# Moving four modulation tiles of layer 2 into an expert stage, with smaller bias tables and a later query factor

## Chip, cores and metric

One core of one Trainium2 chip runs the whole program. The metric is the device time of one execution in microseconds; lower is better. TensorE (PE), VectorE (DVE), ScalarE (ACT), GpSimd (POOL) and SyncE (SP) each run their own instruction stream in order, and wait for one another by semaphores. SP and ACT also issue DMA transfers from their streams.

## What is computed

Two blocks of two layers each work on 256 tokens of 1024 numbers, in float32. Every layer is a mixer (an attention or a gated scan) followed by 16 experts of which each token uses two. In block 1, `c` modulates both halves of a layer:

```
cond = silu(c)
for l in range(2):
    mod = cond @ w_ada[l] + b_ada[l]
    sh1, sc1, g1, sh2, sc2, g2 = split(mod, 6)
    h = layer_norm(x) * (1 + sc1) + sh1
    x = layer_norm(ALPHA * x + g1 * mixer(h), ln1_g[l], ln1_b[l])
    h = layer_norm(x) * (1 + sc2) + sh2
    x = layer_norm(ALPHA * x + g2 * moe(h), ln2_g[l], ln2_b[l])
```

`mod` has 6144 numbers, twelve tiles of 512. Tiles 0 to 3 (`sh1`, `sc1`) are needed when a layer begins. The mixer of block 1 normalizes queries and keys by head, turns them by position ("rope") and scales scores by 1/8. The second layer of block 2 adds a bias by relative position, looked up in a table of 32 buckets, to its scores.

## The kernel before

Everything is unrolled; a scheduler puts each engine's instructions in order. The text order is its priority, `after_last(engine)` keeps an instruction behind the last one written for that engine, and `chain_begins` to `chain_ends` marks stretches that keep the written order. The stages follow one another: layer 1 of block 1, its experts (tag `moe10`), layer 2, its experts (`moe11`), then block 2 with `moe20` and `moe21`.

**A layer of block 1** (`block1`) multiplies the tokens by weights in 28 units: 20 of `w_in`, 4 of the branches, 4 of `w_out`. Weights come as 1 MB tiles into a ring of eight. Each is split into a high part on ACT (`whi`, L346) and a low part on DVE (`wlo`, L356), and a unit is 48 matmuls of 128x128 by 128x256 (L427). After every 12 of these, `Flow.tick` resumes the side tasks: the lane `job` holds rope, `att` the attention, and `ada` the modulation.

**The modulation** of one tile (`ada_task`) loads 2 MB in two transfers on SP's queue, then sums the eight slices of it on DVE into `adac`: one multiplication (L520) and seven multiply-adds (L522). For tiles that are needed as columns, four narrow products on PE (L529) and one addition on DVE (L532) end it; for the gate rows `g1` and `g2` it is one product of 128x512 (L534) and an addition (L536). The lane begins after a pause of 12 ticks (`ADA_START`). In layer 1 it takes tiles 4 to 11 of its own layer, then tiles 0 to 3 of layer 2, then a folding of the router's weights. Before the units of `w_out` the lane is drained: whatever is left of it is written there, in front of the residual. The first `w_out` units are computed by `residual`, with `ot` (L1018) as the first step of its DVE chain, and behind the merged branches (`mt`, L1501 to L1505).

**Rope** (L1296 on) has POOL raise the mean square to the power -1/2 (`rstd_of`, L203). For the queries DVE then multiplies the result `rq` by 0.125 (L1309), ahead of the rotation (`sq` on DVE, `o2` on POOL, `qro` as their sum, L1327) and the transposes (L1333). `rq` itself is used only in the softmax of `global_job`.

**An expert stage** (`moe`) gathers the tokens of four experts at a time (`pg`, L334), then works on pairs of experts: `up` (L786), `act`, `down` (L850), and `land`, which spreads the results (`sc`) and adds them to `X` (L892). Weight tiles of 1 MB are loaded ahead into the ring, into ten more slots of the same size that lie where the layer's own tiles were, and into two work tiles; `PLAN1` gives their order. In the middle of the stage (`OV_AT`) every engine takes a branch (L907) around code for experts with more than 64 tokens. Places marked by `hint_for` tell an engine beforehand where that branch leads; for `moe10` the short engines have one mark, at the very start of the program, and PE has two more inside the stage.

**The bias table** is made by `bias_task` in layer 2: eight rows of 384 numbers, each written 128 times to the DRAM tile `fd` (L1542), so that `diff` can read it back shifted by one number per partition, in two transfers (L1783).

Of the kernel before, what the change touches and what calls it, by code (L numbers as in the profile page):

```python
# [91 lines left out]

RING = 8
TICK = 12
ADA_START = (12, 12)

TAIL_ENG = (ENG.Activation, ENG.PE)
WARM = ((3, 2, 10), (3, 2, 10))
# [7 lines left out]
def _plan(places, fixed):  # L106

    turns = [i for i in range(len(places)) if i not in fixed.values()]
    return [(p, fixed[p] if p in fixed else turns.pop(0)) for p in (("ring" if p == "r" else p) for p in places)]


PLAN1 = _plan([5, 6, 7] + ["r"] * 8 + [9, 8, 1, 2, 3, 4, 0, "yy"], {"yy": 8})
SLOTS1 = (1, 9, PLAN1, 99), (1, 9, PLAN1, 99)
FIX2 = {"sa": 3, "yy": 17}
SLOTS2 = ((3, 8, _plan([3, "r", "r", 8, 9, 4, 5, 6, "r", "r", "r", 7, 10, "r", "r", "r", "yy", 1, 2, 0, "sa", "rows"], FIX2), 14),
          (3, 8, _plan([8, 9, 3, "r", 5] + ["r"] * 7 + [4, 6, 10, 7, "yy", 1, 2, 0, "sa", "rows"], FIX2), 14))
SM_TICKS = 4
JOB_GAP = 2
P_BUFS = 4
S_BANKS = 3  # L120
DEC = 4
TAGS = ("moe10", "moe11", "moe20", "moe21")
# [8 lines left out]
def body(ctx: ExitStack, tc: tile.TileContext, A: dict, out: bass.AP, dbg=None):  # L131
# [377 lines left out]
    def ada_task(ps, pool, l, m, step):  # L509

        src = kview(A["w_ada"][l], m * 512, (m + 1) * 512)
        if m not in MODC:
            b = A["b_ada"][l, m * 512:(m + 1) * 512]
            g = gates[l, m // 6][:, (m % 2) * 512:(m % 2) * 512 + 512]
            S.dma_start(g, bass.AP(tensor=b.tensor, offset=b.offset, ap=[[0, P], [1, 512]]))
        ws = [wload([4, 512], [(None, src[:, 4 * i:4 * i + 4])]) for i in range(2)]
        yield 2
        acc = pool.tile([P, 512], F32, tag="adac", name="adac", bufs=1)
        with after_chain():
            V.tensor_scalar(acc, ws[0][:, 0], ce[:, 0:1], None, op0=OP.mult)  # L520
        for k in range(1, KC):
            V.scalar_tensor_tensor(acc, ws[k // 4][:, k % 4], ce[:, k:k + 1], acc, op0=OP.mult, op1=OP.add)  # L522
            if k % step == 0:
                yield 1
        yield 1
        pa = ps.tile([P, 512], F32, tag="tp", name="pa", bufs=2)
        if m in MODC:
            for j in range(4):
                PE.matmul(pa[:, j:j + 1], acc[:, j * 128:(j + 1) * 128], one32[:, 0:1], start=(j == 0), stop=(j == 3),  # L529
                          skip_group_check=True)  # L530
            yield 1
            V.tensor_tensor(modc[l][:, MODC[m]:MODC[m] + 4], pa[:, 0:4], modc[l][:, MODC[m]:MODC[m] + 4], op=OP.add)  # L532
        else:
            PE.matmul(pa, one32, acc, start=True, stop=True)  # L534
            yield 1
            V.tensor_tensor(g, pa, g, op=OP.add)  # L536


    def rank4(mp, v, n, tag):
# [106 lines left out]
        else:  # L646
            V.tensor_copy(cb[:, 1], pb[:, n:2 * n])

    def moe(z, kind, slots, scored, wg, wu, wd, mod, gate, tag, after, again, reorder=False, room=()):

# [4 lines left out]
        with ExitStack() as es:  # L657
# [298 lines left out]
            gx = gather(0)  # L956
            pos_sb = mo.tile([P, 48], F32, tag="pos", name="pos_sb")
            V.tensor_copy(pos_sb, pos[:, 0:48])
            ga = act(0, *up(0, gx))
            if reorder:  # L960
                with after_last(ENG.Activation):
                    S.dma_start(X, xd.rearrange("(t p) d -> p t d", p=P))
            for pi in range(8):
                if pi in (OV_AT - 3, OV_AT - 1):
                    with after_last(ENG.PE):
                        tc.mark_branch_hint_location("ov" + tag, engines=[ENG.PE])
                if pi < 7:
                    if pi % 2 == 1:
                        gx = gather(pi // 2 + 1)
                    gu = up(pi + 1, gx)  # L970
                st = ga[0]
                ys = down(pi, *ga, pi == 7)
                if pi < 7:
                    ga = act(pi + 1, *gu)
                    land(pi, 0, spread(st, *ys, 0))
                    land(pi, 1, spread(st, *ys, 1))
                if pi == OV_AT:
                    overflow()
                if pi == OV_AT + 1:
                    for e in SHORT:  # L980
                        with after_last(e):
                            hint_for(TAGS[TAGS.index(tag) + 1:], e)
                if pi == 6:
                    with after_last(ENG.Activation):
                        tail = Tail(after(), again)
                    chain_begins(*TAIL_ENG)
# [175 lines left out]
    def block1(l, prev):  # L1162

        with tc.tile_pool(name="gp", bufs=1, reuse_waits="tile") as gp:
            gates[l, 1] = gp.tile([P, D], F32, name="g2")
            es = gp.tile([P, 2, NE], F32, name="es")
            with ExitStack() as stack:
# [128 lines left out]
                def rope(src, dst, H, nm, rs, permute):  # L1296
# [8 lines left out]
                    if not permute:  # L1305
                        sv = src.rearrange("p t (h e) -> p (t h) e", e=64)
                        V.tensor_tensor(sv, sv, rs[:, :, None].to_broadcast([P, 2 * H, 64]), op=OP.mult)
                    else:
                        V.tensor_scalar(rs, rs, 0.125, None, op0=OP.mult)  # L1309
                    tA, tB = tabs[nm]  # L1310
                    o2 = d.tile([P, 2, H * 64], F32, tag="kdT", name="o2")
                    for tt in range(2):
# [12 lines left out]
                        else:  # L1325
                            o, a, b = dst[:, tt], sq[:, tt], o2[:, tt]
                        V.tensor_tensor(o, a, b, op=OP.add)  # L1327
                    for tt in range(2):
                        yield 2
                        if permute:  # L1330
                            pt = ps.tile([P, 512], F32, tag="tp", name="ptq")
                            for j in range(4):
                                PE.transpose(pt[:, j * P:(j + 1) * P], qro[:, tt, j * P:(j + 1) * P], ident)  # L1333
                            S.activation(qT[:, :, tt * P:(tt + 1) * P], pt.rearrange("p (j t) -> p j t", j=4), AF.Copy)
                        else:
                            pt = ps.tile([P, 512], F32, tag="tp", name="ptk")
                            PE.transpose(pt[:, 0:P], kro[:, tt, :], ident)
                            S.activation(kT[:, tt * P:(tt + 1) * P], pt[:, :P], AF.Copy)
# [103 lines left out]
                if ADA_START[l]:  # L1442
                    fl.add("ada", pause(ADA_START[l]))
                fl.add("ada", *[ada_task(ps, d2, l, m, ADA_STEP[l]) for m in range(4, 12)])
                fl.add("ada", *[ada_task(ps, d2, k, m, ADA_STEP[l]) for k in range(l + 1, DEPTH) for m in range(4)])
                fl.add("ada", fold(ps, d2, "adas", route, modc[l][:, 24:32], modc[l][:, 16:24], False))
                if l + 1 == DEPTH:
                    fl.add("ada", bias_task(ps, d2))
# [58 lines left out]
                def logits(tt, t, sd):  # L1507
# [4 lines left out]
                             route, logits, gates[l, 0])  # L1512
            return moe(z, 1, SLOTS1[l], (es, route[1]), A["w_exp_gate"][l], A["w_exp_up"][l], A["w_exp_down"][l],
                       (modc[l][:, 24:32], modc[l][:, 16:24]), gates[l, 1], f"moe1{l}",
                       lambda: rows_of(A["ln2_g"][l], A["ln2_b"][l], False), l + 1 < DEPTH, l + 1 == DEPTH)


    lam = cst.tile([P, 4], F32, name="lam")
    fd = dram.tile([8, P, 384], F32, name="fd")
    fap = fd[:]  # L1520

    def bias_task(ps, pool):
# [16 lines left out]
        yield 1  # L1539
        fsb = pool.tile([8, 384], F32, tag="pT", name="fsb", bufs=3)  # L1540
        V.tensor_copy(fsb, pf[0:8, :384])
        S.dma_start(fd, fsb[:, None, :].to_broadcast([8, P, 384]))  # L1542
        yield 2
        t = pool.tile([P, 128], F32, tag="adas", name="ltm")
        tc.keep_in_program_order(V.tensor_tensor(t, ab[0], ab[1], op=OP.mult))
# [194 lines left out]
    def diff(prev, gp, room, load_router, logits, rows):  # L1740
        with tc.tile_pool(name="dl", bufs=1, reuse_waits="tile") as dl, tc.tile_pool(name="d", bufs=1, reuse_waits="tile") as d, tc.tile_pool(name="d2", bufs=2, reuse_waits="tile") as d2, \
# [38 lines left out]
            v = [t[:, 0].rearrange("p (t n) -> p t n", t=2) for t in vb]  # L1780
            Tb = [t[:, 1].rearrange("p (h n) -> p h n", h=4) for t in vb]
            for i in range(2):
                S.dma_start(Tb[i], bass.AP(tensor=fap.tensor, offset=fap.offset + 127 + i * 4 * P * 384,  # L1783
                                           ap=[[383, P], [P * 384, 4], [1, 256]]))
            pbuf = slot(7, [4, 2, 256], "pbuf")
            pairs = [(0, 1), (2, 3)]
            gs = row_bcast(d, "gs", A["b_g_sub_2"][0])
# [166 lines left out]
```

## Time and profile before

| | us |
|---|---|
| three runs | 1598.65, 1603.44, 1602.59; median 1602.59 |
| the profiled execution | 1602.16 |
| its span, first to last instruction | 1600.4 |
| PE busy | 1470.0 |
| DVE busy | 869.0 |
| ACT busy | 432.8 |

The profiled execution lies 0.4 us below the median, and its span 1.8 us below its time. The mean granted TensorE clock is 0.969 of full speed. By the profile's times, layer 1 runs up to about 277 us, `moe10` to about 430 us, layer 2 to about 674 us and `moe11` to about 840 us.

### The profile page before, as it was taken

Reading aid. Unit: us, or ns where it says so; the run is one execution under the profiler, and the core shown is the slowest. Engines: PE = TensorE matmul, PEld = TensorE weight load, DVE = VectorE, ACT = ScalarE, POOL = GpSimd, SP = SyncE. Lnnn points to the kernel's source line nnn. Section 1 sums busy time; section 2 is a strip of 40 time slices with the busy share of each in tenths; the row PEclk is TensorE's granted clock in tenths of the full one; section 3 lists DMA queues with packets and bytes.
Section 4 is the critical chain, followed back from the end, with each engine's and each line's share of the span. In section 5 each row is a group of like instructions: output and inputs, shape, how many; then the busy total and the mean of one; then the engine's idle time right before and its main releaser. Section 6 shows DMA issues by size and latency. Waiting matters only on the chain. (4 is left out here: it accounts for less than half of the span.)

```text
span 1600.4 us, 22811 instructions
## 1 busy us (share of the span) xinstructions
PE 1470.0 (92%) x9124; PEld 969.4 (61%) x9124; DVE 869.0 (54%) x1686; ACT 432.8 (27%) x733; POOL 129.2 (8%) x140
## 2 busy tenths in 40 slices
PE   4999987998889999889989999999998999999895
PEld 3879987443478999734448895443337988434331
DVE  3689998343678879823464574231127776212214
ACT  1454331211235434111125331110103652101000
POOL 0200002000121000300011001000003002000001
PEclk9999999999979999889999999999999999999998
DMA  9978799995855769799887487999999966999993
GB/s 301 365 249 273 259 303 324 353 302 198 268 174 173 242 232 337 167 363 359 292 263 214 133 290 267 386 387 353 381 334 288 298 195 244 341 386 387 346 386 124
DMA packets 324371, 461.69 MB, mean 288 GB/s; under 512 B 20077, under 2 KB 178285, under 8 KB 324258
## 3 DMA queue, kind: packets, MB, share of 16 engines
q1 hardware_dynamic: 308720, 446.34, 81.5%
q10 hardware_dynamic: 15538, 13.81, 3.5%
q8 instruction: 76, 1.25, 0.3%
q14 instruction: 37, 0.30, 0.1%
HBM read 456.43 MB, written 3.67 MB: 287 GB/s over the span
## 5 line engine op out<-in xcount | busy, mean ns | idle before, releaser
L786 PE MATMUL gu<-w,xg 128*64 128x512 f32 x1536 | 369.2, 597 | 0.0
L786 PEld LDWEIGHTS gu<-w,xg 128*64 128x64 f32 x1536 | 110.8, 137 | 209.1 <-issue 202.7
L356 DVE TENSOR_TENSOR wlo<-w,whi 128x2048 fp32r<-128x2048 f32 (+2 forms) x92 | 183.3, 1994 | 44.9 <-ACT whi L346 44.2
L850 PE MATMUL y<-w,sa 128*64 128x512 f32 x768 | 195.6, 607 | 4.4 <-DMA w<-in_w_exp_down_dram 4.4
L346 ACT ACTIVATE whi<-w 128x2048 fp32r<-128x2048 f32 (+2 forms) x92 | 157.9, 1726 | 151.4 <-PE acc L427 111.6
L850 PEld LDWEIGHTS y<-w,sa 128*64 128x64 f32 x768 | 55.0, 138 | 106.0 <-issue 97.7
L830 DVE SCALAR_TENSOR_TENSOR sa<-gu,cr,sa 128x256 f32<-128x256 f32 (+1 forms) x32 | 19.7, 615 | 163.6 <-PE gu L786 136.4
L334 PE MATMUL sc<-yy,st 128*128 128x512 f32 x256 | 88.8, 436 | 18.1 <-ACT yy L860 14.3
L522 DVE SCALAR_TENSOR_TENSOR adac<-w,ce,adac 128x512 f32<-128x512 f32 x140 | 104.7, 748 | 1.2
L427 PE MATMUL acc<-hl,whi 128*128 128x256 f32 x608 | 93.3, 286 | 0.0
L427 PE MATMUL acc<-hh,whi 128*128 128x256 f32 x608 | 90.4, 289 | 1.6 <-ACT whi L346 1.6
L892 DVE TENSOR_TENSOR x<-x,sc 128x512 f32<-128x512 f32 x112 | 74.3, 683 | 30.4 <-PE sc L334 30.3
L427 PE MATMUL acc<-hh,wlo 128*128 128x256 f32 x608 | 85.9, 281 | 0.0
L334 PE MATMUL pg<-oh,zh 128*128 128x256 f32 x256 | 73.8, 319 | 13.1 <-DVEq L907 7.3
L334 PEld LDWEIGHTS sc<-yy,st 128*128 128x128 f32 x256 | 42.0, 188 | 70.7 <-ACT yy L860 36.0
L427 PEld LDWEIGHTS acc<-hh,whi 128*128 128x128 f32 x608 | 78.4, 190 | 6.8 <-issue 4.1
L427 PE MATMUL acc<-whi,hh 128*128 128x256 f32 x416 | 70.9, 303 | 12.2 <-ACT hh L1240 8.9
L427 PEld LDWEIGHTS acc<-hl,whi 128*128 128x128 f32 x608 | 79.6, 189 | 3.7 <-issue 3.2
L427 PEld LDWEIGHTS acc<-hh,wlo 128*128 128x128 f32 x608 | 77.3, 188 | 1.0 <-issue 0.8
L334 PEld LDWEIGHTS pg<-oh,zh 128*128 128x128 f32 x256 | 55.4, 218 | 27.8 <-issue 15.0
L334 PE MATMUL pg<-oh,zl 128*128 128x256 f32 x256 | 71.2, 308 | 0.9 <-issue 0.9
L860 ACT ACTIVATE yy<-y 128x512 fp32r<-128x512 f32 x32 | 19.1, 597 | 192.2 <-PE y L850 192.2
(376 smaller groups left out, 2107.8 us busy)
## 6 DMA issues: line engine op xcount, KB each, us to landing
w<-in_moe_w_gate_dram SPq DMA_DIRECT2D x64, 1024.0 KB, 12.1
w<-in_moe_w_up_dram SPq DMA_DIRECT2D x64, 1024.0 KB, 13.8
w<-in_moe_w_down_dram SPq DMA_DIRECT2D x128, 512.0 KB, 11.6
w<-in_w_ada_dram SPq DMA_DIRECT2D x47, 1024.0 KB, 7.2
w<-in_w_in_dram SPq DMA_DIRECT2D x40, 1024.0 KB, 5.6
w<-in_w_exp_gate_dram SPq DMA_DIRECT2D x64, 512.0 KB, 9.5
w<-in_w_exp_up_dram SPq DMA_DIRECT2D x64, 512.0 KB, 8.8
w<-in_w_exp_down_dram SPq DMA_DIRECT2D x64, 512.0 KB, 8.9
```

The costliest lines, as they stand in the source:

```text
L334: PE.matmul(dst, l, r, start=(i == 0), stop=(i == n - 1), skip_group_check=True)
L346: S.activation(hi[:, k0:k0 + n], w, AF.Copy)
L356: eng.tensor_tensor(lo[:, k0 + x:k0 + y], w[:, x:y], hi[:, k0 + x:k0 + y].bitcast(F32), op=OP.subtract)
L427: PE.matmul(dst, l, r, start=(start and i == 0), stop=(i == n - 1), skip_group_check=True)
L522: V.scalar_tensor_tensor(acc, ws[k // 4][:, k % 4], ce[:, k:k + 1], acc, op0=OP.mult, op1=OP.add)
L786: PE.matmul(gu[64 * j:64 * j + 64, :], xg[:, 4 * kh + k, (2 * pr + j) * CAP:(2 * pr + j + 1) * CAP], ws[j][:, k, :], start=(kh == 0 and k ...
L830: V.scalar_tensor_tensor(sg, u, cr, sg, op0=OP.mult, op1=OP.mult)
L850: PE.matmul(y[64 * j:64 * j + 64, :], aT[:, f, 64 * j:64 * j + 64], w[:, j, k, :], start=(f == 0), stop=(f == NF - 1), tile_position=(0, 6 ...
L860: S.activation(yh[:, hs], src, AF.Copy)
L892: V.tensor_tensor(X[:, tt, hs], X[:, tt, hs], sc, op=OP.add)
```

## The change

The four tiles of layer 2 leave the `ada` lane of layer 1. `ada_steps` sums them inside `moe10` instead, in 16 steps of two slices, each with a load of 0.5 MB on ACT's queue into one of two new buffers; one call starts it after the first pair, then three calls a pair for pairs 0 to 2 and two for the others. `moe10` gets one slot less ahead. In layer 2 the pause of the lane is 8 ticks in place of 12. In `ada_task` the gate rows' product comes `step` ticks later. The queries' factor stands below the rotation. `moe10` marks the branch once more after pair 1 for DVE, ACT, POOL and SP. Each row of `fd` is written 32 times instead of 128, and read in eight transfers of 32 partitions.

```diff
-ADA_START = (12, 12)
+ADA_START = (12, 8)
...
-SLOTS1 = (1, 9, PLAN1, 99), (1, 9, PLAN1, 99)
+PLAN0 = _plan([5, 6, 7] + ["r"] * 8 + [8, 1, 2, 3, 4, 0, "yy"], {"yy": 8})
+SLOTS1 = (1, 8, PLAN0, 99), (1, 9, PLAN1, 99)
...
+FD = 32
...
@@ ada_task
-        yield 1
+        yield 1 if m in MODC else step + 1
...
+    def ada_steps(ps, pool, l):
+        steps = [(m, i) for m in range(4) for i in range(4)]
+        def load(m, i):
+            w = pool.tile([P, 2, 512], F32, tag="adaw", name="adaw", bufs=2)
+            with after_last(ENG.Activation):
+                S.dma_start(w, kview(A["w_ada"][l], m * 512, (m + 1) * 512)[:, 2 * i:2 * i + 2])
+            return w
+        w = load(*steps[0])
+        yield
+        for n, (m, i) in enumerate(steps):
+            ahead = load(*steps[n + 1]) if n + 1 < len(steps) else None
+            if i == 0:
+                acc = pool.tile([P, 512], F32, tag="adac", name="adac", bufs=1)
+            with after_last(ENG.DVE):
+                for j in range(2):
+                    k = 2 * i + j
+                    if k == 0:
+                        V.tensor_scalar(acc, w[:, 0], ce[:, 0:1], None, op0=OP.mult)
+                    else:
+                        V.scalar_tensor_tensor(acc, w[:, j], ce[:, k:k + 1], acc, op0=OP.mult, op1=OP.add)
+            w = ahead
+            yield
+            if i == 3:
+                pa = ps.tile([P, 512], F32, tag="tp", name="pa", bufs=2)
+                with after_last(ENG.PE):
+                    for j in range(4):
+                        PE.matmul(pa[:, j:j + 1], acc[:, j * 128:(j + 1) * 128], one32[:, 0:1], ...
+                with after_last(ENG.DVE):
+                    V.tensor_tensor(modc[l][:, MODC[m]:MODC[m] + 4], pa[:, 0:4], modc[l][:, MODC[m]:MODC[m] + 4], op=OP.add)
...
@@ moe
+            ada = iter(()) if ada is None else ada_steps(ps, mp, ada)
             ga = act(0, *up(0, gx))
+            next(ada, None)
...
                     land(pi, 1, spread(st, *ys, 1))
+                for _ in range(3 if pi < 3 else 2):
+                    next(ada, None)
+                if pi == 1 and tag == TAGS[0]:
+                    for e in SHORT:
+                        with after_last(e):
+                            hint_for(TAGS, e)
...
@@ rope
-                    else:
-                        V.tensor_scalar(rs, rs, 0.125, None, op0=OP.mult)
...
                         V.tensor_tensor(o, a, b, op=OP.add)
+                    if permute:
+                        V.tensor_scalar(rs, rs, 0.125, None, op0=OP.mult)
...
@@ block1
-                fl.add("ada", *[ada_task(ps, d2, k, m, ADA_STEP[l]) for k in range(l + 1, DEPTH) for m in range(4)])
...
@@ bias_task, diff
-    fd = dram.tile([8, P, 384], F32, name="fd")
+    fd = dram.tile([8, FD, 384], F32, name="fd")
...
-        S.dma_start(fd, fsb[:, None, :].to_broadcast([8, P, 384]))
+        S.dma_start(fd, fsb[:, None, :].to_broadcast([8, FD, 384]))
...
-                S.dma_start(Tb[i], bass.AP(tensor=fap.tensor, offset=fap.offset + 127 + i * 4 * P * 384,
-                                           ap=[[383, P], [P * 384, 4], [1, 256]]))
+                for p0 in range(0, P, FD):
+                    S.dma_start(Tb[i][p0:p0 + FD], bass.AP(tensor=fap.tensor, offset=fap.offset + 127 - p0 + i * 4 * FD * 384,
+                                                           ap=[[383, FD], [FD * 384, 4], [1, 256]]))
```

## Rows read from the trace of the kernel before

**Rows 1.** The page's busy time by engine, whole span.
```profile
PE 1470.0 (92%) x9124; PEld 969.4 (61%) x9124; DVE 869.0 (54%) x1686; ACT 432.8 (27%) x733; POOL 129.2 (8%) x140
```

**Rows 2.** Busy time by stretch: us, engines' busy us (instructions), PEclk, DMA share, GB/s.
```profile
350.00:410.00 60.00, 55.30 (x226) 21.61 (x225) 21.81 (x39) 9.42 (x22) 1.18 (x2) 0.94 0.54 181
210.00:260.00 50.00, 41.38 (x317) 40.03 (x316) 45.84 (x89) 12.25 (x14) 1.53 (x1) 0.93 0.96 315
370.00:390.00 20.00, 15.30 (x66) 8.56 (x67) 7.93 (x14) 3.52 (x6) 1.18 (x2) 0.83 0.83 279
700.00:710.00 10.00, 7.27 (x15) 1.92 (x16) 0.92 (x2) 0.63 (x1) 0.00 (x0) 0.50 1.05 381
```

**Rows 3.** PE's waits, 190 to 252 us: total us, times, longest.
```profile
PE acc L427 <- DVE wlo L356: 2.2, 1, 2.2
PE acc L427 <- ACT mh L1504: 2.1, 1, 2.1
PE accb L427 <- DVE mt L1502: 2.0, 2, 1.6
PE acc L427 <- DVE ot L1018: 1.9, 1, 1.9
```

**Rows 4.** Instructions on the tile `adac`, 185 to 250 us: durations ns min/median/max.
```profile
L522 DVE SCALAR_TENSOR_TENSOR adac<-w,ce,adac x32: 732/747/752, 184.8 to 244.1; 128x512 f32<-128x512 f32 x32
...
L520 DVE TENSOR_SCALAR adac<-w,ce x4: 477/480/485, 191.8 to 233.4; 128x512 f32<-128x512 f32 x4
```

**Rows 5.** PE's waits, 560 to 700 us (end of layer 2's mixer).
```profile
PE acc L427 <- DVE ot L1018: 1.7, 1, 1.7
```

**Rows 6.** PE's waits, 62 to 100 us (layer 1's first units).
```profile
PE ptq L1333 <- DVE qro L1327: 2.7, 1, 2.7
PE pa L534 <- DVE adac L522: 2.2, 1, 2.2
```

**Rows 7.** Waits around the queries' rope: layer 1 (DVE), then layer 2 (PE).
```profile
DVE rq L1309 <- POOL rq L203: 2.1, 1, 2.1
...
PE ptq L1333 <- DVE g L536: 1.7, 1, 1.7
```

**Rows 8.** The branch L907 in `moe10`, and who waited for it.
```profile
L907 DVEq COMPARE_BRANCH x1: 84/84/84, 375.8 to 375.8; - x1
...
L907 DVEq EVENT_SEMAPHORE x1: 21/21/21, 381.1 to 381.1; - x1
...
  PE pg L334: 4.7, 1
```

**Rows 9.** The same branch in `moe11`, 750 to 850 us.
```profile
L907 DVEq COMPARE_BRANCH x1: 74/74/74, 784.4 to 784.4; - x1
L907 DVEq EVENT_SEMAPHORE x1: 21/21/21, 784.9 to 784.9; - x1
```

**Rows 10.** DMA queues, 645 to 680 us: packets, MB, share of 16 engines.
```profile
q10 hardware_dynamic: 1032, 1.57, 36.2%
q1 hardware_dynamic: 3295, 3.38, 31.3%
```

**Rows 11.** PE in order of time in `moe11`: start us, us, what, [idle before].
```profile
701.33 1.94 PE L850 MATMUL y<-w,sa 128*64 128x512 f32 x2 [3.00 <-DMA w<-in_w_exp_down_dram]
704.67 6.37 PE L850 MATMUL y<-w,sa 128*64 128x512 f32 x14 [1.40 <-DMA w<-in_w_exp_down_dram]
```

**Rows 12.** PE in order of time: the same products in `moe10`.
```profile
299.82 3.65 PE L850 MATMUL y<-w,sa 128*64 128x512 f32 x16
```

**Rows 13.** All DMA in `moe10`, 280 to 350 us.
```profile
DMA packets 20557, 24.92 MB, mean 356 GB/s; under 512 B 757, under 2 KB 16070, under 8 KB 20554
```

**Rows 14.** DVE in order of time in `moe10`, [idle before].
```profile
333.66 0.42 DVE L822 TENSOR_SCALAR st<-pst 128x256 fp32r<-128x256 f32 x1 [5.54 <-ACT pst L821]
```

**Rows 15.** DMA issues of the whole run: count, KB each, us to landing.
```profile
rows<-in_ln_b_dram ACTq DMA_DIRECT2D x6, 512.0 KB, 7.4
```

**Rows 16.** The two reads of `fd` (L1783): durations ns.
```profile
L1783 ACTq DMA_DIRECT2D vb<-fd x2: 378/379/380, 1178.6 to 1182.0; - x2
```

More of the change, by code (lines that the diff above doesn't have):

```diff
@@ L536, in ada_task @@
             V.tensor_tensor(g, pa, g, op=OP.add)
+    def ada_steps(ps, pool, l):
[24 more added lines that the diff above has]
+                    for j in range(4):
+                        PE.matmul(pa[:, j:j + 1], acc[:, j * 128:(j + 1) * 128], one32[:, 0:1], start=(j == 0), stop=(j == 3),
+                                  skip_group_check=True)
+                with after_last(ENG.DVE):
+                    V.tensor_tensor(modc[l][:, MODC[m]:MODC[m] + 4], pa[:, 0:4], modc[l][:, MODC[m]:MODC[m] + 4], op=OP.add)
     def rank4(mp, v, n, tag):
@@ L647, in fold, with moe @@
             V.tensor_copy(cb[:, 1], pb[:, n:2 * n])
-    def moe(z, kind, slots, scored, wg, wu, wd, mod, gate, tag, after, again, reorder=False, room=()):
+    def moe(z, kind, slots, scored, wg, wu, wd, mod, gate, tag, after, again, reorder=False, room=(), ada=None):
         F = wg.shape[2]
@@ L1514, in block1 @@
                        (modc[l][:, 24:32], modc[l][:, 16:24]), gates[l, 1], f"moe1{l}",
-                       lambda: rows_of(A["ln2_g"][l], A["ln2_b"][l], False), l + 1 < DEPTH, l + 1 == DEPTH)
+                       lambda: rows_of(A["ln2_g"][l], A["ln2_b"][l], False), l + 1 < DEPTH, l + 1 == DEPTH,
+                       ada=l + 1 if l + 1 < DEPTH else None)
     lam = cst.tile([P, 4], F32, name="lam")
-    fd = dram.tile([8, P, 384], F32, name="fd")
+    fd = dram.tile([8, FD, 384], F32, name="fd")
     fap = fd[:]
```

## The prediction

> **What bounds the kernel now.** I read the page's busy times first: PE is busy for 1470.0 of 1600.4 us, DVE for half of that [rows 1]. The kernel is bound by PE, so only PE's gaps, and stretches in which it runs below full clock, can be shortened. The next views are therefore PE's waits stage by stage, then for each gap the engine named as its releaser, in order of time, and the DMA queues where a transfer is the releaser. Four places matter.
>
> At the end of layer 1's mixer PE has gaps of 2.2, 2.1, 2.0 and 1.9 us [rows 3]. In those 50 us DVE is busy for 45.84 us, PE for 41.38, and PE's mean granted clock is 0.93 [rows 2]. Four sums of modulation tiles begin in that stretch [rows 4]; by the order of the lane they are the four of layer 2, which the drain has put in front of the residual. DVE is the bound here, for a moment.
>
> In the first units of layer 1, PE waits 2.2 us for a gate row's sum and 2.7 us for the rotated queries [rows 6], and DVE in turn had stood 2.1 us at `rq`, for POOL's power; at the same place of layer 2 PE has a gap of 1.7 us [rows 7].
>
> In `moe10` the branch costs DVE 5.3 us, from 375.8 to 381.1, and PE waits 4.7 us for what stands behind it [rows 8]. The same branch takes 0.5 us in `moe11` [rows 9].
>
> In `moe11` PE waits 3.0 and 1.4 us for one tile of `w_exp_down`, and its products then run at the lower level (granted 0.50, so 1.2 GHz) [rows 2, 11]. Just before, the write of `fd` is in flight: over 35 us ACT's queue took 36.2% of the DMA engines for 1.57 MB, while the weights in SP's queue got 3.38 MB through [rows 10]. At the rate of `moe10`, 356 GB/s [rows 13], 35 us carry 12.5 MB; only 5.0 MB moved.
>
> **The change part by part.** *The four tiles leave layer 1.* A tile costs DVE 0.48 + 7 x 0.747 = 5.7 us, four 22.8 us [rows 4], and an addition each. That is half of DVE's 45.84 us in the stretch, so DVE stops being the bound there. The PE gaps sum to 8.2 us. Layer 2's mixer ends in the same way with only its last gate tiles draining, and still shows a gap of 1.7 us [rows 5]; I leave that much, and take 6.5. The clock loss there is 0.07 x 41.38 = 2.9 us [rows 2]; part of it is owed to gaps that stay behind 250 us, so I take 1.5. Together 8.0, between 3 (DVE's splitting of weights is late without them too) and 11. The lane of layer 1 now has 12 + 4 x 7 + 4 x 9 + 2 = 78 ticks against 88 that the units give, so little is drained; before it was 98. The eight loads of 1 MB leave SP's queue, and `w_out` and the experts behind them can only come sooner.
>
> *Gate products later, the factor below the rotation.* In layer 1 the 2.2 us wait for the gate's sum goes, since the product is issued two ticks later. `rq` no longer stands ahead of `qro`, so 2.1 of the 2.7 us go; POOL has ended its power by the time that the rotation's last sum is done, and nothing waits for `rq` until the softmax. Sum 4.3, taken as 4.0, bounds 0 and 5. In layer 2 the 1.7 us gap goes: 1.5, bounds 0 and 2. What is late next is DVE itself, busy nearly throughout. Layer 2's lane starts 4 ticks sooner and each of its four gate rows ends a tick later, so it ends where it did: 0, within 1.5 either way.
>
> *The second mark for the branch.* If it does for `moe10` what the mark set a stage ahead does for `moe11`, DVE's 5.3 us become 0.5. PE's wait falls from 4.7 us to about 0.3, a gain of 4.4, and of the clock loss, 0.17 x 15.30 = 2.6 us [rows 2], about half goes, since it follows that gap: 5.5, bounds 0 and 7. Four marks cost an instruction each on engines that have room.
>
> *A quarter of `fd`.* The write fell on 36.2% of 16 engines for 35 us; a quarter of the packets is about 9 us of this, so the weights behind it come some 20 us sooner. PE could have begun the products at 701.33 - 3.00 = 698.3 and ended at 711.0, 12.7 us; in `moe10` the same sixteen take 3.65 [rows 11, 12]. The difference, 9.1 us, is the most to be had; I take 8, with 2 as the lower end in case the slot of that tile, and not the queue, holds it back. The reads become eight: six more issues of 0.38 us on ACT, 2.3 us in a stage where ACT mostly waits [rows 16]: cost 0.5, bounds 0 and 2.
>
> *The tiles' sums in `moe10`.* PE's work is only moved: the narrow products of a tile are taken from layer 1 and added here, net 0. The loads, 16 of 0.5 MB or 8.4 MB, cost 8.4 / 356 GB/s = 23.6 us of DMA [rows 13]. From 350 to 410 us the DMA share is 0.54 [rows 2], so 0.46 x 60 = 27.6 us lie free there, more than the loads need. That the engines could rest so long, while no weights are named among `moe10`'s waits, means that weights run that far ahead of PE; loads that come in before 350 us only use up this lead. They are hidden; if that cover failed, the price would be up to 23.6 us. One prefetch slot less, in other places: cost 1, bounds 0 and 3, since SP's queue is in order and a slot that comes free late holds those behind it.
>
> DVE has 22.8 us more to do, while PE computes `up`. Its gap there is 5.5 us in a pair [rows 14], and three steps of two slices take 3 x 1.5 = 4.5. But there are two buffers: the load of a burst's third step must wait on ACT until DVE has done the first. The nearest row for a 0.5 MB load from ACT's queue lands in 7.4 us [rows 15], so the third step could end 1.5 + 7.4 + 1.5 = 10.4 us into the gap, 4.9 late. What queues behind it on DVE is the next pair's `st`, `sa`, `yt` and `yy`, for which PE waits; behind the waiting load on ACT stand the next pair's Silu and its copies of `yy`. Three bursts are of three steps: bounds 0 (the scheduler puts the next pair's work ahead, or the load lands in the gap) and 14.7. A burst of two finds its second load issued ahead of the gap. I take 1 us for each of the three, 3 in all, because the scheduler orders by when it thinks data is ready.
>
> **Sum.** 8.0 + 4.0 + 1.5 + 5.5 + 8.0 - 0.5 - 1.0 - 3.0 = 22.5 us off the profiled execution's 1602.2: 1579.7. That execution lies 0.4 below the median, so the forecast for the median is **1580**.
>
> **The rivals.** *The mark changes nothing.* DVE's branch in `moe10` is missed though a mark was set, at the program's start, and the new one still stands some two pairs ahead of the branch. Against: in `moe11` a mark set longer before works [rows 9]. Then 5.5 us are lost: 1585.
> The Trainium skill (Runtime: NRT & Kernel Launch, section Instruction fetch mechanics) says that instructions are fetched one page after the other into a window of two, and that a taken branch out of that window waits for a fetch; by that rule a mark far ahead could keep nothing, and the time would be this rival's. The 0.5 us of `moe11`'s branch speaks against it as far as it goes.
>
> *The third steps are late.* All three cost their 4.9 us, and the gaps lower the clock as at 700 us, so 14.7 in place of 3: about 1592.
>
> *Slower.* The loads in ACT's queue land late for every burst: the three of three steps and the four of two. The mechanism is DVE's order: a multiply-add that waits for its load holds the next pair's `sa` and `yy`, and PE stops in every pair. All other terms give 25.5 us, so it decides from 25.5 / 7 = 3.6 us a burst. At the bound of 4.9 it costs 34 us: 1611. For it: the DMA share near 1 up to 350 us. Against: weights of the same size pass at 356 GB/s then, and DVE is idle for most of each pair.
>
> *The change doesn't free PE.* If the gaps at the end of layer 1 only move to the next wait (first loads of `moe10`, routing) and the tile of `moe11` stays late, 3 + 0 + 0 + 0 + 2 less the costs of 4.5 is about 0: 1601.
>
> **How the numbers follow.** The forecast has 0.56, the dead mark 0.24, late third steps 0.10, no freed PE 0.05, slower 0.05. About 0.3%, 5 us, is what a measurement of this kernel can tell from no change, so the line lies at 1597.8. The first three cases are faster, but for a small share of the late steps: 0.88. Within 0.3%: 0.07. Slower by more: 0.05. At their best all terms give 11 + 5 + 2 + 7 + 9.1 = 34 us, 1568. The range reaches from 1569, nearly that, to 1594, past the dead mark and the late steps; it leaves out the last two cases and a tail below, under 2 in 10.
>
> **What would show it.** In the profile of the changed kernel: no `adac` sums after about 215 us in layer 1 and no PE gap over 1 us before `ot`; `rq` behind `qro`, without DVE's wait; DVE's branch in `moe10` within 1 us; ACT's queue with about 260 packets instead of 1032 after the end of layer 2's mixer, and the sixteen products of `moe11`'s first `down` in 3.65 us. PE's waits within `moe10`, now none, tell how late the steps are. I am wrong if gaps of several us appear there in each pair, or if `moe10` begins no sooner than 277 us.

## The result and the profile after

| | before | after |
|---|---|---|
| median, us | 1603.0 (4 runs, 1598.65 to 1605.08) | 1582.9 (4 runs, 1581.69 to 1584.21) |
| profiled execution, its span | 1602.16, 1600.4 | 1581.69, 1579.9 |

The ratio is 0.988, with a 95% interval from 0.986 to 0.990: 20 us faster. Forecast were 1580, with 1569 to 1594 as the range. The total is near; its parts are less so. The table takes the first gate product and the last down product of each expert stage from both traces; a gain is positive. The prediction's terms stand beside it.

| stretch | before, ends at | after, ends at | gain | forecast |
|---|---|---|---|---|
| layer 1, to `moe10`'s first gate product | 280.6 | 260.9 | 19.7 | 8.0 + 4.0 |
| `moe10`, to its last down product | 419.1 | 404.9 | -5.5 | 5.5 - 1.0 - 3.0 |
| layer 2, to `moe11`'s first gate product | 677.2 | 663.9 | -0.9 | 1.5 |
| `moe11`, to its last down product | 822.6 | 799.2 | 10.1 | 8.0 |
| mixer, to `moe20`'s first gate product | 978.6 | 955.1 | 0.1 | 0 |
| `moe20`, to its last down product | 1204.6 | 1184.8 | -3.7 | -0.5 |
| the rest | 1600.4 | 1579.9 | 0.7 | 0 |

Each length in the table is from one trace, and traces scatter. Nine kernels, this one among them, have the same code up to there and begin `moe10` between 257.6 and 261.6 us; `moe10` takes 144.0 us here and 146.3, 146.7 and 147.0 in three kernels that differ from this one elsewhere or by a mark alone; the mixer of block 2 takes 154.3 to 160.6 us over all kernels. A difference of 2 or 3 us between two stages is therefore not told by two traces, unless a wait shows it.

Busy times of the kernel after, from the page, against [rows 1]: PE is busy for 9 us less with the same number of instructions. The mean granted clock went from 0.969 to 0.974, which for 1470 us of PE is an estimate of 7.5 us.

```profile
PE 1461.2 (92%) x9124; PEld 964.1 (61%) x9124; DVE 869.2 (55%) x1686; ACT 431.9 (27%) x733; POOL 132.1 (8%) x140
```

The same columns as in [rows 2], after: the end of layer 1's mixer (20 us earlier now), `moe10` from 350 us, its branch, and the first `down` of `moe11`.

```profile
190.00:240.00 50.00, 49.03 (x411) 48.15 (x411) 40.74 (x76) 17.88 (x22) 1.53 (x1) 1.00 0.87 285
350.00:410.00 60.00, 54.31 (x233) 23.27 (x230) 30.89 (x54) 9.61 (x21) 1.74 (x2) 0.97 0.98 331
360.00:380.00 20.00, 15.46 (x77) 9.12 (x78) 8.96 (x16) 3.29 (x6) 1.74 (x2) 0.91 0.87 297
683.00:693.00 10.00, 10.00 (x53) 5.83 (x53) 7.43 (x14) 3.22 (x7) 1.23 (x2) 1.00 1.10 350
```

Layer 1 ends at full clock with PE busy for 49.03 of 50 us. From 350 to 410 us the DMA share has gone from 0.54 to 0.98. As the stages are shifted, the last 60 us of `moe10` in either kernel compare better: 0.64 before, 1.00 after. The transfers of the new loads are there, and no time lies free. PE's waits at the end of layer 1 (190 to 252 us) and in its first units (62 to 100 us), against [rows 3] and [rows 6]:

```profile
PE rp L1089 <- ACT hTr L1083: 1.0, 2, 0.7
PE acc L429 <- DVE ml L1548: 0.7, 1, 0.7
PE acc L429 <- ACT mh L1547: 0.3, 1, 0.3
...
PE ptq L1377 <- DVE qro L1369: 1.7, 2, 1.0
PE pa L536 <- DVE adac L524: 1.3, 1, 1.3
```

The four gaps of about 2 us are gone. At rope the two gaps are shorter, not gone (4.9 us in all before, 3.0 after); DVE still stands 0.9 us at `rq` between two halves of the rotation. In layer 2 the 1.7 us of [rows 7] has gone, and one of 1.9 us has come elsewhere:

```profile
PE s L1390 <- ACT p L1401: 1.9, 1, 1.9
```

The branch in `moe10`, against [rows 8], and PE's wait behind it:

```profile
L943 DVEq COMPARE_BRANCH  x1: 84/84/84, 366.9 to 366.9; - x1
L943 DVEq EVENT_SEMAPHORE  x1: 21/21/21, 370.1 to 370.1; - x1
...
PE pg L336 <- DVEq L943: 4.5, 1, 4.5
```

DVE's 5.3 us became 3.2, but PE waits 4.5 us where it waited 4.7. In `moe11` the sixteen products of [rows 11] run as one group, and the queues around the write of `fd` (627 to 662 us, against [rows 10]) show a quarter of its packets in q10:

```profile
683.92 3.65 PE L886 MATMUL y<-w,sa 128*64 128x512 f32 x16
...
q1 hardware_dynamic: 8282, 10.07, 87.1%
q10 hardware_dynamic: 264, 0.39, 7.8%
```

Two things are new. In `moe10`, ACT, in order of time, after pair 1: three loads hold it for 10 us, and DVE's sum and the next pair's `st` come late with it (second fence: DVE).

```profile
303.57 10.10 ACTq L547 DMA_DIRECT2D adaw<-in_w_ada_dram  x3
314.99 0.37 ACT L857 ACTIVATE pst<-pst 128x256 f32<-128x256 f32 x1 [10.84 <-DMA adaw<-in_w_ada_dram]
```

```profile
316.60 0.75 DVE L562 SCALAR_TENSOR_TENSOR adac<-adaw,ce,adac 128x512 f32<-128x512 f32 x1 [3.40 <-DMA adaw<-in_w_ada_dram]
317.27 0.42 DVE L858 TENSOR_SCALAR st<-pst 128x256 fp32r<-128x256 f32 x1
```

At the end of `moe20` SP's queue (1120 to 1200 us) waits for the eight reads of `fd`, and PE (1140 to 1190 us) for weights that SP loads behind them. Before, SP's waits on `vb` came to 13.4 us, and PE had no such wait.

```profile
SPq L195 <- DMA vb<-fd: 20.4, 5, 11.8
...
PE y L886 <- DMA w<-in_moe_w_down_dram: 2.3, 3, 0.8
```

### The profile page after: what moved, and what is told of

Its sections match the earlier page's. It is cut to its first block, busy times and chain, and to the rows that moved or that the text cites. A ratio compares the mean times of both kernels' runs of the same rounds, so it can differ in the third digit from the quotient of the medians.

```text
span 1579.9 us, 22833 instructions
## 1 busy us (share of the span) xinstructions
PE 1461.2 (92%) x9124; PEld 964.1 (61%) x9124; DVE 869.2 (55%) x1686; ACT 431.9 (27%) x733; POOL 132.1 (8%) x140
## 5 line engine op out<-in xcount | busy, mean ns | idle before, releaser
L866 DVE SCALAR_TENSOR_TENSOR sa<-gu,cr,sa 128x256 f32<-128x256 f32 (+1 forms) x32 | 19.7, 615 | 163.6 <-PE gu L822 136.3
L336 PE MATMUL sc<-yy,st 128*128 128x512 f32 x256 | 89.2, 437 | 19.7 <-ACT yy L896 13.4
L524 DVE SCALAR_TENSOR_TENSOR adac<-w,ce,adac 128x512 f32<-128x512 f32 x112 | 83.9, 749 | 1.2
## 6 DMA issues: line engine op xcount, KB each, us to landing
w<-in_moe_w_gate_dram SPq DMA_DIRECT2D x64, 1024.0 KB, 12.1
w<-in_moe_w_down_dram SPq DMA_DIRECT2D x128, 512.0 KB, 11.3
```

Of the source, the lines that this page charges most:

```text
L336: PE.matmul(dst, l, r, start=(i == 0), stop=(i == n - 1), skip_group_check=True)
L866: V.scalar_tensor_tensor(sg, u, cr, sg, op0=OP.mult, op1=OP.mult)
```

## The experiments

Medians are of four or more runs; each ratio is to the kernel before, run beside it. Edits are to the changed kernel, 1582.9 us, where nothing else is said.

**The second mark out.** 

```diff
-                if pi == 1 and tag == TAGS[0]:
-                    for e in SHORT:
-                        with after_last(e):
-                            hint_for(TAGS, e)
```

> The second mark for the branch in moe10 is taken out again (DVE, ACT, POOL, SP); all else is the changed kernel. In the changed kernel DVE's branch took 3.2 us there (5.3 before), while PE still waited 4.5 us (4.7 before). Theory A, the mark changes nothing that PE waits for: DVE's branch goes back to about 5.3 us, PE's wait stays at 4.5 within 0.5, the median stays at 1582.9 within 1.5 us. Theory B, the mark shortened DVE's branch and PE's wait is only seen elsewhere: 2 us slower, about 1585. Theory C, the prediction's term: 5.5 us slower, about 1588.

1584.2 us, 0.988 [0.985, 0.991]. DVE's branch takes 3.2 us and PE waits 4.5, both as with the mark. So in this kernel the mark changes nothing at the branch; theory A, but the 3.2 us were not its work either.

**`fd` written 128 times, read twice.** `FD = 128`.

> Each row of fd is written 128 times again and read in two transfers; all else is the changed kernel. Theory A, the shorter write gives moe11 its gain and the eight reads hold up the weights at the end of moe20: moe11 (from its first gate product to its last down product) 10 us longer, PE's waits of 3.0 and 1.4 us for w_exp_down are back, moe20 about 3 us shorter without its three waits for w_moe_down; about 1589.5. Theory B, moe11 gained by something else (order of the stage before, layer 2 starting sooner): moe11 as in the changed kernel, moe20 3 us shorter, about 1580. Theory C, the reads cost nothing and moe20 lost by the order of its loads: 1593.

1591.5 us, 0.992 [0.989, 0.995]. PE's waits in `moe11` (667 to 820 us):

```profile
PE y L886 <- DMA w<-in_w_exp_down_dram: 7.0, 2, 5.4
```

`moe11` takes 146.5 us against 135.4, `moe20` 225.9 against 229.7, and PE's waits for `w_moe_down` are gone. Theory A: the short write is worth 11 us, the eight reads cost 3.8.

**The tiles in layer 1 again.** 

```diff
-SLOTS1 = (1, 8, PLAN0, 99), (1, 9, PLAN1, 99)
+SLOTS1 = (1, 9, PLAN1, 99), (1, 9, PLAN1, 99)
...
+                fl.add("ada", *[ada_task(ps, d2, k, m, ADA_STEP[l]) for k in range(l + 1, DEPTH) for m in range(4)])
...
-                       ada=l + 1 if l + 1 < DEPTH else None)
```

> The four tiles of layer 2 are summed in layer 1's lane again and moe10 has its ninth slot back; all else is the changed kernel (gate products later, factor below the rotation, second mark, short fd). Theory A, the move is what freed layer 1: moe10's first gate product about 15 us later (19.7 less some 4 for the products' other places), moe10 itself 5 to 7 us shorter than in the changed kernel, so in all 8 to 10 us slower, about 1592. Theory B, layer 1 gained mostly by the other places of the gate product and the factor: first gate product at most 8 us later, moe10 5 us shorter, about 1586. Theory C, the move gives nothing in the end, moe10 loses what layer 1 gains: 1583 within 2.

1586.1 us, 0.989 [0.986, 0.992]: only 3 us slower, and the two intervals overlap, so what the move as such gives in the changed kernel is not told from nothing; most of what layer 1 gains is paid elsewhere. Some 17 of the 20 us are there without the move. Layer 1 does lose what theory A says, and more: the first gate product comes at 278.8 us, 17.9 later. But `moe10` takes 132.7 us in place of 144.0, less than before the change (138.5). DVE's branch there takes 0.6 us. The stage as a row of busy times (PE's busy time is the second number), in this kernel, in the changed one and in the kernel before:

```profile
278.80:411.50 132.70, 132.39 (x585) 53.49 (x584) 55.41 (x102) 25.65 (x55) 3.55 (x6) 0.99 0.87 291
```

```profile
260.90:404.90 144.00, 135.99 (x608) 57.24 (x608) 75.53 (x138) 25.02 (x54) 4.10 (x6) 0.99 0.96 325
```

```profile
280.60:419.10 138.50, 133.80 (x585) 55.02 (x584) 55.40 (x103) 25.68 (x55) 3.55 (x6) 0.98 0.84 281
```

PE's idle time is 0.3 us here, 8.0 in the changed kernel, 4.7 before. Of the 11.3 us between the first two, 3.6 are busy time, as PE has the narrow products of the tiles here (24 of the 32, 3.2 us; the last eight come at 406 us, behind the stage), which took 3.9 us in layer 1; 4.2 are the branch (4.5 against 0.3); 3.5 are other idle time, of which these waits for a late DVE are 3.1:

```profile
PE sc L336 <- DVE yy L897: 1.1, 1, 1.1
PE pat L869 <- DVE sa L866: 1.0, 1, 1.0
PE sc L336 <- DVE x L928: 0.6, 1, 0.6
PE pg L336 <- DVE xg L798: 0.4, 1, 0.4
```

**The steps' loads in POOL's queue**, one for each slice.

```diff
-            with after_last(ENG.Activation):
-                S.dma_start(w, kview(A["w_ada"][l], m * 512, (m + 1) * 512)[:, 2 * i:2 * i + 2])
+            with after_last(ENG.Pool):
+                for j in range(2):
+                    G.dma_start(w[:, j], kview(A["w_ada"][l], m * 512, (m + 1) * 512)[:, 2 * i + j])
```

> The loads of the steps in moe10 are issued in POOL's queue, one for each slice, in place of ACT's; all else is the changed kernel. In the changed kernel ACT issued 16 such loads in order among its Silus and copies, each waiting for a completion counter that it shares with the weights' loads in SP's queue and for DVE to free the buffer; after pair 1 three of them held ACT for over 10 us. Theory A, this order on ACT is what cost moe10 its 5.6 us: ACT's wait of 10.8 us goes, moe10 (144.0 us from first gate product to last down product) gets 4 to 6 us shorter, about 1578. Theory B, DVE's 22.8 us of sums or the slot less are the cost: moe10 within 1.5 us of 144.0, the time within 2 of 1582.9. Theory C, loads in POOL's queue land later, so the steps come later: moe10 longer by 3 us or more, 1586 or above.

1615.0 us, 1.007 [1.005, 1.010], beyond theory C. POOL's row (255 to 440 us; the last numbers are idle time before the issues, the largest part with nothing to wait for), then DVE's wait:

```profile
L548 POOL DMA_DIRECT2D adaw<-in_w_ada_dram x32 | 17.8, 558 | 139.4 <-issue 120.7 <-DVE adac L563 14.5 <-DVE yy L898 2.7
...
DVE adac L563 <- DMA adaw<-in_w_ada_dram: 37.0, 12, 6.0
```

The issuing itself is slow: 120.7 us over 27 of the 32 issues, 4.5 each. The Trainium skill (DMA: Bandwidth & Descriptors, section Anatomy of one DMA — SWDGE (gpsimd) path) fits 2.0 us plus a part by size for a transfer from that queue, from which 2.6 us for one of 256 KB would be an estimate; in this run the median from issue to landing is 4.9 us. `moe10` grew by 33.9 us. It shows what the slower rival described, sums that wait for late loads throughout the stage, though by another queue than the rival's; the prediction put that at 34 us.

**The reads of `fd` in POOL's queue.** `G.dma_start` for `S.dma_start`.

> The eight reads of fd are issued in POOL's queue in place of ACT's; all else is the changed kernel. moe20, from first gate product to last down product, took 226.0 us before, 229.7 in the changed kernel, 225.9 with two reads and the whole write. Theory A, on ACT's queue the eight reads take the eight completion counters in turn with SP's loads, so that w_moe_down waits for reads that wait for a slot to come free: with POOL's own queue SP's waits on vb go, PE's three waits for w_moe_down go, moe20 about 226, the time 3 to 4 us lower, about 1579. Theory B, the reads as such take the DMA's time wherever they are issued: moe20 stays at 229.7, 1583. Theory C, POOL's issues (2.7 to 6 us each in the run before) bring the table late and the scores of the next stage wait: above 1584.

1611.7 us, 1.008 [1.005, 1.012]. `moe20` does take 226.0 us, and SP's waits on `vb` are gone: A's mechanism holds. But the eight issues last from 1155.2 to 1200.7 us, POOL's broadcast of the norm's rows stands behind them, and PE waits for that:

```profile
PE pt L323 <- DVE x L304: 31.9, 1, 31.9
```

**Tiles in layer 1, loads kept in `moe10` with no reader.** The edit with the tiles in layer 1, but `PLAN0` and the 16 loads stay, and the sums and products of `ada_steps` go.

> The four tiles are summed in layer 1's lane again, as in the run with the tiles in layer 1; but moe10 keeps the slot less and issues the same 16 loads on ACT's queue at the same places, with nothing that reads them. It tells the loads and the slot from DVE's sums. moe10 took 132.7 us with the tiles in layer 1, 144.0 in the changed kernel. Theory A, the cost of the steps is DVE's (its sums, and the waits of ACT's loads for DVE to free a buffer): moe10 132.7 to 134.5, DVE's branch 0.6 us, the time about 1586. Theory B, the loads (their counters, their DMA time) or the slot less are the cost: moe10 139 to 144 and the time about 1593. Theory C, half and half: moe10 about 138.

1594.0 us, 0.995 [0.994, 0.997], theories B and C: `moe10` takes 137.6 us.

```profile
275.80:413.40 137.60, 135.28 (x585) 54.18 (x584) 55.24 (x103) 25.28 (x55) 3.56 (x6) 0.99 0.96 327
```

So the loads and the slot less cost 4.9 us on their own, 2.0 as idle time; which of the slot, the bytes and the counters it is, was not told apart. The time as a whole is 7.9 us longer, 6.0 of it in block 2's mixer, which this edit doesn't touch, and layer 1 is 3.0 us shorter. SP's queue waited 50.8 us for these loads in all, as this row from 275 to 415 us shows.

```profile
SPq L195 <- DMA adaw<-in_w_ada_dram: 50.8, 14, 9.1
```

That an SP load waits for a load of ACT's queue is in the program: every transfer of either queue takes one of eight completion counters, and a transfer is issued only when the one that had its counter before has landed. This listing of SP's loads at the end of `moe20` in the changed kernel shows the gaps that the reads of `fd` fill (counters 4, 6, 0, 2 here):

```
L195 DMA w<-in_moe_w_down_dram 128x2x512 [waits DMAHW3_49,PE_49]
L195 DMA w<-in_moe_w_down_dram 128x2x512 [waits DMAHW5_49]
L195 DMA w<-in_moe_w_down_dram 128x2x512 [waits DMAHW7_49,PE_49]
L195 DMA w<-in_moe_w_down_dram 128x2x512 [waits DMAHW1_49]
L195 DMA w<-in_moe_w_down_dram 128x2x512 [waits DMAHW3_49,PE_49]
```

The reads wait for PE to leave their slots, and the loads that take their counters next wait with them, though their own slots are free.

**The steps spread**, no two calls side by side.

```diff
+                next(ada, None)
                 st = ga[0]
...
                     land(pi, 0, spread(st, *ys, 0))
+                    if pi < 3:
+                        next(ada, None)
                     land(pi, 1, spread(st, *ys, 1))
-                for _ in range(3 if pi < 3 else 2):
-                    next(ada, None)
+                next(ada, None)
```

> The 18 calls stay, but they are spread over each pair: one behind the up products, one between the two halves of land (pairs 0 to 2 only), one at the end of the pair; no burst of two or three. All else is the changed kernel. Theory A, bursts make ACT wait with a load for DVE to free a buffer, and that is most of the 11 us that the steps cost moe10: ACT's wait of 10.8 us at pst goes, moe10 gets 4 to 8 us shorter (136 to 140), about 1577. Theory B, the cost is where DVE's multiply-adds stand, however they are grouped: moe10 within 2 of 144, about 1583. Theory C, a call behind up puts sums in front of sa and st for every pair: moe10 longer than 146, 1585 or more.

1575.9 us, 0.984 [0.982, 0.986], theory A (the interval just overlaps the changed kernel's, from 0.986 to 0.990): ACT's wait of 10.8 us is gone, DVE's branch takes 0.5 us, and `moe10` 139.7 us, with 1.8 idle.

```profile
258.20:397.90 139.70, 137.89 (x617) 57.31 (x616) 76.41 (x138) 25.54 (x55) 4.09 (x6) 0.99 0.96 324
```

PE's idle time in the stage falls by 6.2 us, and 4.2 of this are the branch's. The run with three small parts undone (below) bears this out: it keeps the bursts and ACT's wait of 10.8 us, its branch is as short as here, and PE is idle for 4.0 us in 142.0. So about 4 of the 6.2 us come with the branch and about 2 with the spreading; the branch's part may be no work of the spreading, as the account of the second mark shows. The median is 7 us lower, the profiled execution only 3.7, with the stage 4.3 us shorter; the rest is not accounted for.

**The mark after pair 3.** `if pi == 3` for `if pi == 1`.

> The second mark stands after pair 3 in place of pair 1 (on DVE 19 instructions ahead of the branch in place of 54); all else is the changed kernel. DVE's branch in moe10 took 0.6 us with the mark and no steps between (40 instructions ahead), 3.2 with the mark and the steps, 3.2 with the steps and no second mark. Theory A, what is run between the mark and the branch decides, and a mark near the branch holds: DVE's branch 0.6, PE's wait of 4.5 us falls to about 1.5, the time about 3 us lower, 1580. Theory B, with the steps the mark does nothing wherever it stands: 3.2 us, 4.5 us, 1583. Theory C, so near to the branch the fetch has not ended: 1 to 3 us, about 1581.5.

1580.4 us, 0.988 [0.985, 0.991]: no difference that can be told. DVE's branch takes 2.5 us and PE waits 3.9, in theory C's bounds; that the fetch has not ended so near the branch was not shown.

**Three small parts undone.** `ADA_START = (12, 12)`, `yield 1` in `ada_task`, the factor above the rotation.

> Three small parts are undone together: the gate rows' product comes as early as before, the queries' factor of 0.125 stands above the rotation, and layer 2's lane begins after 12 ticks; all else is the changed kernel. Theory A, the prediction's terms: layer 1's gate wait of 2.2 us and most of the 2.7 us for qro come back, and in layer 2 the gap of 1.7 us: 4.0 + 1.5 us slower, about 1588.4. Theory B, the run with the tiles back in layer 1 began moe10 at 278.8 us against 280.6 before, so the parts are worth some 1.8 us in layer 1 and little in layer 2 (changed kernel 259.0 us from moe10's last down to moe11's first gate product, 258.1 before): about 1585. Theory C, nothing: 1583.

1580.9 us, 0.985 [0.982, 0.988], theory C in the time. Yet layer 1 shows theory A: its waits are back to 2.7 and 2.2 us and `moe10` begins 5.3 us later, at 266.2. Most of this is given back: `moe10` is 2.0 us shorter, with a branch of 0.6 us and a wait of 1.5 in place of 4.5 behind it; layer 2 is 1.1 us shorter, within its scatter. At the profile's end 1.6 us are left. Nothing in this edit touches the branch.

**Spread steps, reads behind `hh4`**: `with after_last(ENG.Activation)` around the reads.

> The spread steps, and the eight reads of fd are pinned behind the last instruction of ACT written before them (the copies of moe20's result into hh4), still on ACT's queue; then no read waits for a slot and none stands among the loads of w_moe_down. With the spread steps alone: 1575.9 us, moe20 228.1 us, w_moe_down's loads waiting for vb. Theory A, the reads cost by the completion counters that they share with the loads while they wait for a slot: SP's waits on vb go, PE's waits for w_moe_down go, moe20 about 226, the time 2 to 4 us lower, about 1573. Theory B, eight issues of 0.44 us in front of ACT's splitting of the next weights cost as much there: 1575 to 1577. Theory C, the table lands late for the next stage's scores: 1579 or above.

1588.9 us, 0.991 [0.988, 0.995]. `moe20` takes 226.0 us without waits for weights, as A says, but B's cost is far larger than B said: the eight reads hold ACT for 7.8 us from 1193.3 us on, where it splits the next weights.

```profile
PE acc L429 <- ACT whi L348: 10.8, 1, 10.8
```

**Spread steps, one tile in layer 1**: tile 0 as an `ada_task` of layer 1's lane, `range(1, 4)` in `ada_steps`.

> The spread steps with three tiles in moe10; tile 0 of layer 2 goes back to layer 1's lane, which then has 78 + 9 = 87 of the 88 ticks of its units, so that it needs no drain. Theory A, what cost layer 1 was the drain in front of the residual, 10 ticks beyond the units: one tile costs layer 1 at most 2 us and spares moe10 a quarter of the 7 us that the spread steps cost it: 1574 to 1576, moe10 about 138, its first gate product at 260 us or below. Theory B, each tile costs layer 1 a quarter of the 17.9 us, since DVE is busy throughout: first gate product near 263, about 1578.5.

1581.9 us, 0.985 [0.982, 0.988]. The interval overlaps that of the spread steps alone. The first gate product comes at 262.7 us, near theory B (the three kernels with spread steps and no tile in layer 1 have 258.3, 260.3 and 259.8), and `moe10` gains nothing that can be told (140.3 us against 139.6, 141.1 and 138.9). So a lane that fits its ticks did not spare layer 1 this; by one trace it is no more than a hint that ticks are not the measure.

**Spread steps, `FD = 64`.**

> The spread steps, and 64 copies of each row of fd in place of 32, so four reads in place of eight; all else as in the run with the spread steps (1575.9 us, moe11 136.5 us from first gate product to last down product, moe20 228.1). With 128 copies and two reads moe11 took 146.5 and moe20 225.9. Theory A, the weights behind the write have slack for half of it and each read costs on its own: moe11 within 1 us of 136.5, moe20 about 227, the time 1574 to 1576. Theory B, the write's cost is in proportion to its length, 10 us for 96 copies: moe11 about 140, moe20 about 227, 1578. Theory C, four reads hold the loads as long as eight, since all wait for the same slot: moe20 228 to 230, 1576 with no cost in moe11, 1580 with.

1575.1 us, 0.982 [0.981, 0.984], the lowest here, not told apart from the spread steps alone, but below the changed kernel's interval. `moe11` takes 135.3 us: half the write costs nothing that can be told. Four reads hold `moe20` as long as eight did (228.6 us; 227.8 to 229.9 with eight), theory C:

```profile
PE y L886 <- DMA w<-in_moe_w_down_dram: 2.0, 2, 1.7
```

## Why the prediction was right, and where its steps were not

*The four tiles leave layer 1* (8.0, bounds 3 to 11): right, and too small. With the small parts undone `moe10` begins at 266.2 us against 280.6, so the tiles are worth 14.4, give or take 2. The 32 narrow products took 4.1 us of PE there, which the prediction had set against the same in `moe10`; the other 10.3 are at the upper bound. The waits at the end of the mixer fell from 8.2 us to 2.0, by 6.2, near the 6.5 that were taken. What is left, some 4 us, is by difference the clock, of which 1.5 had been taken: after, the granted clock is 1.00, so 2.4 GHz, from 190 to 240 us, where it was 0.93 before. One reading was wrong: not half of DVE's 45.84 us from 210 to 260 us was work on `adac`, but 12.1 us, as the four sums began at 191.8 us [rows 4]; all 22.8 us lie between 190 and 252 us. With the tiles back in layer 1, gap after gap, it is a mix of the two levels, 0.76 on average from 240 to 260 us:

```profile
240.00:260.00 20.00, 17.48 (x113) 17.10 (x113) 16.64 (x37) 1.19 (x2) 1.53 (x1) 0.76 1.07 339
```

*Gate products and factor in layer 1* (4.0): right in sign, 5.3 by one trace (4.6 to 8.6 by the scatter) where DVE is free behind them; the two named waits themselves fell by 1.9 us, not by the 4.3 of the sum, as DVE still stands at `rq`. With the tiles still in the lane 1.8 is left (278.8 against 280.6), which two traces don't tell from nothing. *Layer 2* (1.5): nothing; the wait moved from `ptq` to the softmax.

*The second mark* (5.5): failed in this kernel, with the first rival's outcome: 0.2 us at PE. The step took it that a mark makes the branch short, and no run shows this. With the tiles in layer 1 the branch took 0.6 us, PE's idle time fell from 4.7 to 0.3, and the stage got 5.8 us shorter; but no run takes the mark out of a kernel whose branch is short. Of the kernels with the second mark, eight show 0.5 or 0.6 us and four 2.5 to 3.2; the two without it show 5.3 and 3.2. The distance to the mark doesn't sort them: in the kernel before, it stands 508 of DVE's instructions ahead in `moe10` (5.3 us) and 497 ahead in `moe11` (0.5 us, [rows 9]). Nor does the order of instructions that the steps make: with the three small parts undone, all that DVE runs in `moe10` up to the branch is the same, in the same order, as in the changed kernel, and yet:

```profile
L943 DVEq COMPARE_BRANCH  x1: 84/84/84, 374.3 to 374.3; - x1
L943 DVEq EVENT_SEMAPHORE  x1: 21/21/21, 374.9 to 374.9; - x1
```

What does sort all fourteen kernels is how many records DVE's stream has ahead of the branch, waits for semaphores counted: 575 or 576 in the six with a long branch, 573 or 580 and more in the eight with a short one. The traces also show a transfer in it: in each of the six long branches one or two loads of 8 KB begin in a queue of instructions (q14) while DVE stands there, and in none of the eight short ones. In the changed kernel, from 366.9 to 370.2 us (queue: packets, MB, share of 16 engines):

```profile
q14 instruction: 2, 0.02, 1.7%
```

The Trainium skill (Runtime: NRT & Kernel Launch, section Instruction fetch mechanics) says that a branch out of a window of two pages waits for a fetch; the long branches, with these loads in them, are in accord with that. The short ones, with the mark near or 497 instructions ahead, are not explained by it. Why the place in the stream should decide, and whether the mark has any part in it, stays open; a kernel that only shifts the branch by a few instructions would tell.

*A quarter of `fd`* (8.0, at most 9.1): right in its mechanism, with 10.1 above its own upper bound, and 11.1 by the run that undoes it, as the tile then waits 7.0 us. *Eight reads* (0.5, bounds 0 to 2): 3.7. The step priced the issues on ACT, 2.3 us; the price was in SP's queue, by the shared counters: `moe20` is back at 226.0 us in both runs that take the reads out from among SP's loads.

*DVE's steps in `moe10`* (3.0): right in size, 3.1 by PE's waits for a late DVE; the waiting third load that the step described is seen after pair 1 alone, as ACT's wait of 10.8 us. *The loads hidden, one slot less* (0 and 1.0): the run with loads that nobody reads puts both at up to 4.9. Free DMA time was there (0.54), but the loads took SP's counters as well as bytes, and the step had no term for the counters.

So the total was right by luck, by terms that made up for one another: layer 1 gave 7.7 us more than said, of which 4.1 came back as products (3.2 in `moe10`, the rest just behind it), and `moe11` 2.1 more; the mark, the reads and layer 2 gave 5.3, 3.2 and 2.4 less. `moe10` lost 5.5 us: 3.3 more of PE's idle time and 2.2 of its busy time, so that of the 3.2 us of products there some 1.0 were made up, it seems by the clock (0.98 before, 0.99 after).

## What to carry to other kernels

Work moved out of a stage that an engine bounds can free more than its own gaps: here 6.2 us of waits and 4.1 of products went, and the granted clock rose from 0.93 to 1.00. But where the work goes, it costs its products, its loads and the order of the queue that issues them; as first written the move gained nothing that can be told, and with its steps spread about 10 us (1586.1 to 1575.9). Give a transfer that must wait for a buffer or a slot its own place: neither in a burst, nor in a queue whose next instruction the critical engine needs, nor among prefetches with which it shares counters. Splitting two transfers into eight multiplies the counters they hold, not only the issues. And a wait that comes and goes with edits that don't touch it, as at this branch, must be read in every trace before its time is booked to an edit.

## What was not expected of the hardware

- Transfers issued by POOL came 2.7 to 7.5 us after the last one, with nothing else to wait for that the profile shows, whereas an issue in ACT's queue took 0.37 us. Eight such reads kept POOL from 1155.2 to 1200.7 us.
- A branch past the same code cost DVE between 0.5 and 5.3 us in one stage. With the same instructions in the same order throughout that stage it took 3.2 us in one kernel and 0.6 in another, which had three waits for semaphores fewer in DVE's stream ahead of it; 8 KB loads of instructions began within the long branches only.
